# A retention layer's values and gates as one Strassen product whose weight sums are made by adding loads

## The chip, the cores and the metric

One of the eight cores of a Trainium2 chip runs the whole program. The time is that of the device from the start of an execution to its end, in microseconds (us); each run executes the program once, and the median of three runs is quoted. One further execution was recorded by the hardware profiler, and all rows below are from it. TensorE multiplies, VectorE (DVE) and ScalarE (ACT) do arithmetic on tiles, GpSimd (POOL) does arithmetic more slowly and can issue transfers, SyncE (SP) only issues transfers. On TensorE the profile keeps the loading of the stationary operand (PEld) apart from the matmuls (PE).

## The reference

The model has four layers over 512 tokens of width 1024; each has a token mixer and a feed-forward part. Only the mixer of layer 1, a retention with 4 heads, is touched:

```python
proj = x @ w_in                                   # 1024 -> 6144
q, k = proj[..., :1024], proj[..., 1024:2048]     # 4 heads x 256, both rotated
v = proj[..., 2048:4096]                          # 4 heads x 512
g = proj[..., 4096:]                              # 4 heads x 512
y = (retention_chunked(q, k, v, log_gamma[0], False)
     + flip_seq(retention_chunked(flip_seq(q), flip_seq(k), flip_seq(v), log_gamma[1], True)))
y = (y - mean(y)) * rsqrt(var(y) + eps)           # over the 512 columns of a head
y = y * gn_w + gn_b
return (silu(g) * y) @ w_o                        # 2048 -> 1024
```

All of it is in 32-bit floats.

## The kernel before, in words

Tokens lie in 4 tiles of 128. The layer's input stands transposed in `xh` and `xl`: every 32-bit operand of a product is split into a rounded high part and the rest (`split`, lines 100 to 103: a copy on ScalarE, line 101, and a subtraction on VectorE, line 102), and `mm3` (lines 124 to 128) multiplies two split operands with three matmuls, high by high, and the two mixed ones. A matmul takes 128 rows by 512 columns.

Weights come through `wload` (lines 105 to 113): SP loads 512 KB into one of three `wraw` tiles, and `wsplit` makes `whi` and `wlo`, of which six pairs exist. For 512 columns a tile holds 2 of the 8 blocks of the inner dimension.

Per head, `retention` does these steps, in this order from head 1 on: `queries_keys` (two products of 48 matmuls; the rotation `rope`, lines 778 to 792, is six operations on VectorE and two splits for each), `turn` (line 904: 16 transposes of the gated result of the head before, four splits), `values` (96 matmuls, split as they leave PSUM), `scores` (24 matmuls, the decay on VectorE, splits), `gate` (96 matmuls, Silu on ScalarE), `mix` (line 881: 48 matmuls, then for each token tile the group norm) and `out` (line 915: 96 matmuls with the output weights of the head before, added into the residual `xt`). After head 3, `turn` and `out` are done once more, and the layer norm follows.

The group norm of a tile is statistics on VectorE (lines 893 and 894), a reciprocal root by eight small operations (`rsqrt`, lines 139 to 147), one more small operation (898), the scaling on ScalarE (899), the product with the weights on VectorE (900), and the addition of the bias and the product with the gate on GpSimd (901 and 902).

The order of each engine's instructions is fixed when the program is built. The framework goes by the order of the code, but passes over an instruction whose buffer or operand isn't ready in its own model of the times and takes a later one that is. On the chip every engine runs its instructions in that order, and waits where something is late. Buffers of general use (`b`, 2 KB per partition) are 47 in this layer; PSUM has 6 banks for products and 2 for transposes.

## Time and profile before

| | |
|---|---|
| median of 3 runs | 2554.17 us (2553.12 to 2557.45) |
| the profiled execution, own time | 2556.36 us |
| its span in the profile | 2554.6 us |
| TensorE busy, share of the span | 99% |
| VectorE, ScalarE, GpSimd | 69%, 38%, 8% |
| mean granted clock of TensorE | 0.996 of full |
| retention layer | about 594 to 1028 us of the span |

The own time of the profiled execution counts 1.8 us that lie outside the first and last instruction of the span. Matmuls overlap in the profile, so that the time from the start of one to the start of the next says what each costs, not its duration. An engine's busy share says nothing of when it waits; the timeline does.

### The profile page before, as it was taken

How to read it: one execution, taken by the hardware profiler on the slowest of the kernel's cores; microseconds unless marked ns; L12 is line 12 of the kernel's file. 1: busy time of each engine (PE TensorE's matmuls, PEld its weight loads, DVE VectorE, ACT ScalarE, POOL GpSimd, SP SyncE). 2: the span in 40 equal slices, each digit the busy share in tenths (PEclk: the TensorE clock that was granted, in tenths of full speed). 3: DMA queues.
4: the chain of work that ended last, by engine and by line, in shares of the span. 5: the costliest groups of instructions: out<-in, count | busy, mean ns of one | idle time of the engine just before them, and what ended most of it. 6: DMA issues, size and time to landing. Idle time of an engine off the chain costs nothing.

```text
span 2554.6 us, 32573 instructions
## 1 busy us (share of the span) xinstructions
PE 2528.1 (99%) x12804; PEld 2151.0 (84%) x12804; DVE 1771.5 (69%) x2988; ACT 975.2 (38%) x1405; POOL 200.8 (8%) x247
## 2 busy tenths in 40 slices
PE   8999999999999999999999999999999999999998
PEld 7888888888888888988888899988888888988887
DVE  6887766658655647666657878866657786666656
ACT  4653333323332323333332665233332564233331
POOL 2000111000101101111100000011100100011101
PEclk9999999999999999999999999999999999999999
DMA  4213333323222323333333322333332221333331
GB/s 149 75 42 95 99 105 101 99 83 99 77 89 66 97 94 99 99 99 99 107 99 83 91 73 75 112 99 99 99 91 79 83 67 58 109 99 99 99 91 58
DMA packets 294713, 232.35 MB, mean 91 GB/s; under 512 B 21120, under 2 KB 244480, under 8 KB 294560
## 3 DMA queue, kind: packets, MB, share of 16 engines
q1 hardware_dynamic: 294560, 230.28, 29.9%
q8 instruction: 100, 1.64, 0.3%
q14 instruction: 53, 0.43, 0.1%
HBM read 228.15 MB, written 2.10 MB: 90 GB/s over the span
## 4 chain that ended last, share of the span: by engine, by line
PE 93%; DVE 3%; ACT 2%; DMA 1%; issue 1%; POOL 1%; SPq 0%; DVEq 0%; ACTq 0%
PE ps L126 30%; PE ps L128 30%; PE ps L127 30%; PE tp L658 1%; PE tp L156 1%; DVE wlo L102 1%; PE ps L639 1%; PE ps L638 1%; DMA wraw<-in_mla_w_down 0%; ACT whi L101 0%; DMA wraw<-in_ret_w_in 0%; ACT bh L101 0%; DVE xt L203 0%; DVE lnst L184 0%; DVE xt L180 0%
## 5 line engine op out<-in xcount | busy, mean ns | idle before, releaser
L101 ACT CAST whi<-wraw 128x1024 fp32r<-128x1024 f32 (+3 forms) x398 | 412.0, 1040 | 693.7 <-PE ps L127 228.8
L126 PE MATMUL ps<-xh,whi 128*128 128x512 f32 (+1 forms) x1792 | 656.8, 367 | 0.0
L127 PE MATMUL ps<-xl,whi 128*128 128x512 f32 (+1 forms) x1792 | 656.5, 366 | 0.1
L128 PE MATMUL ps<-xh,wlo 128*128 128x512 f32 (+1 forms) x1792 | 656.4, 366 | 0.0
L102 DVE TENSOR_TENSOR wlo<-wraw,whi 128x1024 fp32r<-128x1024 f32 (+3 forms) x398 | 487.8, 1235 | 211.6 <-ACT whi L101 204.3
L127 PEld LDWEIGHTS ps<-xl,whi 128*128 128x128 f32 x1792 | 337.9, 189 | 55.1 <-DVE lnx L139 0.3
L128 PEld LDWEIGHTS ps<-xh,wlo 128*128 128x128 f32 x1792 | 337.9, 189 | 54.9
L126 PEld LDWEIGHTS ps<-xh,whi 128*128 128x128 f32 x1792 | 337.6, 189 | 55.1 <-issue 0.4
L126 PE MATMUL ps<-whi,xh 128*128 128x512 f32 (+3 forms) x752 | 265.1, 353 | 0.7 <-ACT xh L101 0.7
L128 PE MATMUL ps<-whi,xl 128*128 128x512 f32 (+3 forms) x752 | 263.2, 350 | 1.6 <-DVE xl L102 1.5
L127 PE MATMUL ps<-wlo,xh 128*128 128x512 f32 (+3 forms) x752 | 262.9, 350 | 0.3 <-DVE lnx L139 0.2
L180 DVE TENSOR_TENSOR xt<-ps,xt 128x512 f32<-128x512 f32 x288 | 187.2, 682 | 34.9 <-PE ps L128 34.9
L126 PE MATMUL ps<-whi,fh 128*128 128x512 f32 x448 | 174.3, 389 | 0.0
L127 PE MATMUL ps<-wlo,fh 128*128 128x512 f32 x448 | 174.3, 389 | 0.0
L128 PE MATMUL ps<-whi,fl 128*128 128x512 f32 x448 | 174.3, 389 | 0.0
L128 PEld LDWEIGHTS ps<-whi,xl 128*128 128x128 f32 x752 | 143.2, 190 | 19.9 <-DVE xl L102 2.9
L126 PEld LDWEIGHTS ps<-whi,xh 128*128 128x128 f32 x752 | 143.4, 191 | 18.4 <-ACT xh L101 1.1
L127 PEld LDWEIGHTS ps<-wlo,xh 128*128 128x128 f32 x752 | 143.3, 191 | 17.5 <-DVE wlo L102 0.9
L322 DVE TENSOR_TENSOR ft<-ps,b 128x512 f32<-128x512 f32 x64 | 44.2, 691 | 141.5 <-PE ps L128 77.9
L101 ACT CAST whi<-wt 128x1024 fp32r<-128x1024 f32 x64 | 67.5, 1054 | 191.4 <-PE ps L127 131.3
L325 POOL TENSOR_TENSOR ft<-ft 128x256 f32<-128x256 f32 x32 | 23.6, 736 | 1485.7 <-DVE ft L322 1485.7
L102 DVE TENSOR_TENSOR fl<-ft,fh 128x1792 fp32r<-128x1792 f32 x32 | 64.8, 2026 | 91.4 <-ACT fh L101 91.4
(257 smaller groups left out, 3989.2 us busy)
## 6 DMA issues: line engine op xcount, KB each, us to landing
wraw<-in_ffn_w_in SPq DMA_DIRECT2D x176, 512.0 KB, 3.9
wt<-in_ffn_w_out SPq DMA_DIRECT2D x48, 512.0 KB, 4.7
wraw<-in_ret_w_in SPq DMA_DIRECT2D x48, 512.0 KB, 3.8
wraw<-in_ffn_w_out SPq DMA_DIRECT2D x40, 512.0 KB, 3.3
wraw<-in_gla_w_in SPq DMA_DIRECT2D x22, 512.0 KB, 3.7
wraw<-in_mla_w_o SPq DMA_DIRECT2D x16, 512.0 KB, 3.8
wraw<-in_ret_w_o SPq DMA_DIRECT2D x16, 512.0 KB, 4.9
wraw<-in_mla_w_down SPq DMA_DIRECT2D x8, 512.0 KB, 4.7
```

The lines of the kernel that those rows point to most:

```text
L101: a = self.nc.scalar.copy(hi, src)
L102: b = self.nc.vector.tensor_tensor(lo, src, hi.bitcast(F32), op=ALU.subtract)
L126: mm(out, s[0], m[0], start=start, stop=False)
L127: mm(out, s[0], m[1], start=False, stop=False)
L128: mm(out, s[1], m[0], start=False, stop=stop)
L156: nc.tensor.transpose(ps[:, j, :], self.xt[t][:, (4 * g + j) * P : (4 * g + j + 1) * P], self.ident)
L180: nc.vector.tensor_tensor(x, ps, x, op=ALU.add)
L322: nc.vector.tensor_tensor(ft[:, 2:4, :] if f % 2 else ft[:, 1::-1, :], half(pu), half(s), op=ALU.mult)
L325: tt(ft[:, 4, :], ft[:, 0, :], ft[:, 3, :], op=ALU.add)
L638: nc.tensor.matmul(ps, qr[:, sl], krh, start=False, stop=False)
L639: nc.tensor.matmul(ps, qr[:, sl], krz[e], start=False, stop=True)
L658: nc.tensor.transpose(ps[:, kk, qq, :], pq[qq][:, k * P : (k + 1) * P], self.ident)
```

## The change

In heads 1 to 3, values and gates become one product of a 512 x 1024 by a 1024 x 1024 matrix, cut into 2 x 2 blocks (256 tokens, 512 of the inner dimension, 512 columns; values are the left column of blocks, gates the right one) and done by Strassen's scheme in Winograd's form with seven block products. The sums of blocks of x are made once per layer on VectorE (`factors`). The sums of weight blocks are made by the transfers: SP loads the first block into a scratch tile, and GpSimd issues up to three more transfers that add to it. The output of the head before is given out in eight steps, two after each of the first four products, and the output of head 3 stays last. The group norm is done for two token tiles together, with all of its tile arithmetic on VectorE. The tags of the layer's buffers change to 30 general ones, 8 for the factors and 2 of scratch.

```diff
--- before.py
+++ after.py
@@ -144,6 +144,23 @@
         stt(u, u, -10.0 / 3.0, u, op0=ALU.add, op1=ALU.mult)
         stt(y, u, 5.0, y, op0=ALU.add, op1=ALU.mult)
         stt(u, y, y, m, op0=ALU.mult, op1=ALU.mult)
+        stt(y, u, 0.5625, y, op0=ALU.add, op1=ALU.mult)
+        return y
+
+    def rsqrt_n(self, v, n, eps, tag):
+
+        tt, ts, stt = self.nc.vector.tensor_tensor, self.nc.vector.tensor_scalar, self.nc.vector.scalar_tensor_tensor
+        x, y, u, m = (self.small(n, tag + c) for c in "xyum")
+        c = -27.0 / 1024.0
+        ts(x, v, eps, None, op0=ALU.add)
+        ts(m, x, c, None, op0=ALU.mult)
+        ts(y.bitcast(I32), x.bitcast(I32), -0.5, float(0x5F3759DF), op0=ALU.mult, op1=ALU.add)
+        tt(u, y, y, op=ALU.mult)
+        tt(u, u, x, op=ALU.mult)
+        stt(u, u, -10.0 / 3.0, u, op0=ALU.add, op1=ALU.mult)
+        stt(y, u, 5.0, y, op0=ALU.add, op1=ALU.mult)
+        tt(u, y, y, op=ALU.mult)
+        tt(u, u, m, op=ALU.mult)
         stt(y, u, 0.5625, y, op0=ALU.add, op1=ALU.mult)
         return y
 
@@ -883,23 +900,28 @@
             gb = self.b()
             nc.sync.dma_start(gw, ins["ret_gn_w"][j, h * 512 : (h + 1) * 512].partition_broadcast(P))
             nc.sync.dma_start(gb, ins["ret_gn_b"][j, h * 512 : (h + 1) * 512].partition_broadcast(P))
-            for t in range(NT):
-                ps = self.ps()
-                sl = slice(t * P, (t + 1) * P)
-                for m in range(NT):
-                    self.mm3(ps, (at[m][0][:, sl], at[m][1][:, sl]), v[m], m == 0, m == NT - 1)
-                st = self.small(6, "gnst")
-                mv = self.small(2, "gnmv")
-                nc.vector.bn_stats(st, ps)
-                nc.vector.bn_aggr(mv, st)
-                r = self.rsqrt(mv[:, 1:2], 1.0, LN_EPS, "gn")
-                y = self.b()
-                nb = self.small(1, "gnb")
-                nc.vector.scalar_tensor_tensor(nb, mv[:, 0:1], -1.0, r, op0=ALU.mult, op1=ALU.mult)
-                nc.scalar.activation(y, ps, AF.Identity, bias=nb, scale=r)
-                nc.vector.tensor_tensor(y, y, gw, op=ALU.mult)
-                nc.gpsimd.tensor_tensor(y, y, gb, op=ALU.add)
-                nc.gpsimd.tensor_tensor(gs[t], gs[t], y, op=ALU.mult)
+            for t0 in (0, 2):
+                pss = []
+                mv = self.small(4, "gnmv").rearrange("p (t a) -> p t a", a=2)
+                for t in (t0, t0 + 1):
+                    ps = self.ps()
+                    sl = slice(t * P, (t + 1) * P)
+                    for m in range(NT):
+                        self.mm3(ps, (at[m][0][:, sl], at[m][1][:, sl]), v[m], m == 0, m == NT - 1)
+                    st = self.small(6, "gnst")
+                    nc.vector.bn_stats(st, ps)
+                    nc.vector.bn_aggr(mv[:, t - t0, :], st)
+                    pss.append(ps)
+                r = self.rsqrt_n(mv[:, :, 1], 2, LN_EPS, "gn")
+                nb = self.small(2, "gnb")
+                nc.vector.scalar_tensor_tensor(nb, mv[:, :, 0], -1.0, r, op0=ALU.mult, op1=ALU.mult)
+                for t, ps in zip((t0, t0 + 1), pss):
+                    e = t - t0
+                    y = self.b()
+                    nc.scalar.activation(y, ps, AF.Identity, bias=nb[:, e : e + 1], scale=r[:, e : e + 1])
+                    nc.vector.tensor_tensor(y, y, gw, op=ALU.mult)
+                    nc.vector.tensor_tensor(y, y, gb, op=ALU.add)
+                    nc.vector.tensor_tensor(gs[t], gs[t], y, op=ALU.mult)
 
         def turn(gs):
             yT = []
@@ -913,11 +935,143 @@
             return yT
 
         def out(h, yT):
-            last = h == RET_H - 1
-            if last:
-                self.ln_begin(l, 0)
+
+            ch = {}
+
+            def step(t, hf):
+                if t == 0:
+                    rows = wo[h * 512 : (h + 1) * 512]
+                    ch[hf] = [self.wcols(rows, c * 256, 2, hf * 512, 512) for c in range(2)]
+                ps = self.ps()
+                for f in range(4):
+                    w2 = ch[hf][f // 2]
+                    sl = slice(t * P, (t + 1) * P)
+                    self.mm3(
+                        ps, (yT[f][0][:, sl], yT[f][1][:, sl]), (w2[0][:, f % 2, :], w2[1][:, f % 2, :]), f == 0, f == 3
+                    )
+                self.acc(t, hf, ps, ALPHA if h == 0 else None, False)
+
+            return [lambda t=t, hf=hf: step(t, hf) for hf in range(2) for t in range(NT)]
+
+        def out_last(h, yT):
+            self.ln_begin(l, 0)
             st = lambda f, t: (yT[f][0][:, t * P : (t + 1) * P], yT[f][1][:, t * P : (t + 1) * P])
-            self.out_proj(st, wo[h * 512 : (h + 1) * 512], 4, ALPHA if h == 0 else None, last)
+            self.out_proj(st, wo[h * 512 : (h + 1) * 512], 4, None, True)
+
+        def factors():
+
+
+            q = [[[x[:, 4 * c : 4 * c + 4, 256 * a : 256 * a + 256] for x in (self.xh, self.xl)] for c in range(2)] for a in range(2)]
+            (a11, a12), (a21, a22) = q
+            f32 = lambda a: a.bitcast(F32)
+            tt = nc.vector.tensor_tensor
+            scratch = lambda: self.b((P, 4, 256), tag="t", name="xs")
+
+            def both(x, y):
+                d, e = scratch(), scratch()
+                tt(d, f32(x[0]), f32(y[0]), op=ALU.subtract)
+                tt(e, f32(x[1]), f32(y[1]), op=ALU.subtract)
+                tt(d, d, e, op=ALU.add)
+                return d
+
+            def keep(d):
+                pr = self.bpair((P, 4, 256), tag="s")
+                self.split(*pr, d)
+                return pr
+
+            d = both(a21, a22)
+            s1 = keep(d)
+            for x in a11:
+                tt(d, d, f32(x), op=ALU.subtract)
+            s2 = keep(d)
+            for x in a12:
+                tt(d, d, f32(x), op=ALU.add)
+            s4 = keep(d)
+            return s1, s2, keep(both(a11, a21)), s4, a11, a12, a22
+
+        def values_gate(h, fac):
+
+
+
+            rows = w.rearrange("(g a p) c -> g p a c", g=4, p=P)
+            s1, s2, s3, s4, a11, a12, a22 = fac
+            v, gs = [None] * NT, [None] * NT
+            tmp = {}
+
+            def load(blocks, c):
+
+                src = [rows[2 * (ac // 2) + c, :, :, 2048 + ac % 2 * 2048 + h * 512 :][:, :, :512] for ac in blocks]
+                if len(blocks) == 1:
+                    t = self.wp.tile([P, 2, 512], F32, tag="wraw", name="wraw", bufs=self.nraw)
+                else:
+                    t = self.b((P, 2, 512), name="wt", tag="t")
+                nc.sync.dma_start(t, src[0])
+                for x in src[1:]:
+                    nc.gpsimd.dma_start(t, x, accum_op=ALU.add)
+                return self.wsplit(t, 2, 512)
+
+            def product(blocks, s, put):
+                ws = [load(blocks, c) for c in range(2)]
+                for tt in range(2):
+                    ps = self.ps()
+                    for k in range(4):
+                        hi, lo = ws[k // 2]
+                        s2_ = tuple(x[:, k, tt * P : (tt + 1) * P] for x in s)
+                        self.mm3(ps, s2_, (hi[:, k % 2, :], lo[:, k % 2, :]), k == 0, k == 3)
+                    put(tt, ps)
+
+            tt_ = nc.vector.tensor_tensor
+
+            def keep(name):
+                def put(tt, ps):
+                    tmp[name, tt] = self.b()
+                    nc.scalar.copy(tmp[name, tt], ps)
+
+                return put
+
+            def put_v(t, x):
+                v[t] = self.bpair()
+                self.split(*v[t], x)
+
+            def put6(tt, ps):
+                u = tmp["u", tt] = self.b()
+                tt_(u, ps, tmp["c11", tt], op=ALU.add)
+                x = tmp["c21", tt]
+                tt_(x, x, u, op=ALU.add)
+
+            def put2(tt, ps):
+                x = tmp["c11", tt]
+                tt_(x, ps, x, op=ALU.add)
+                put_v(tt, x)
+
+            def put5(tt, ps):
+                u = tmp["u", tt]
+                tt_(u, ps, u, op=ALU.subtract)
+
+            def put3(tt, ps):
+                g = gs[tt] = self.b()
+                tt_(g, ps, tmp["u", tt], op=ALU.add)
+                nc.scalar.activation(g, g, AF.Silu)
+
+            def put7(tt, ps):
+                x = tmp["c21", tt]
+                tt_(x, ps, x, op=ALU.add)
+                put_v(2 + tt, x)
+                g = gs[2 + tt] = tmp["u", tt]
+                tt_(g, g, ps, op=ALU.subtract)
+                nc.scalar.activation(g, g, AF.Silu)
+
+            b11, b12, b21, b22 = range(4)
+            steps = [
+                ([b21, b22, b12, b11], a22, keep("c21")),
+                ([b11], a11, keep("c11")),
+                ([b22, b12, b11], s2, put6),
+                ([b21], a12, put2),
+                ([b12, b11], s1, put5),
+                ([b22], s4, put3),
+                ([b12, b22], s3, put7),
+            ]
+            return v, gs, [lambda a=a: product(*a) for a in steps]
 
         for h in range(RET_H):
             if h == 0:
@@ -928,19 +1082,22 @@
                 q, k = queries_keys(h)
                 gs = gate(h)
                 at = scores(h, q, k, gam)
+                gam = decay(1)
+                fac = factors()
             else:
                 q, k = queries_keys(h)
                 yT = turn(gs)
-                v = values(h)
                 at = scores(h, q, k, gam)
                 gam = decay(h + 1) if h + 1 < RET_H else None
-                gs = gate(h)
-            if h == 0:
-                gam = decay(1)
+                v, gs, todo = values_gate(h, fac)
+                outs = out(h - 1, yT)
+                for step in todo:
+                    step()
+                    for _ in range(2):
+                        if outs:
+                            outs.pop(0)()
             mix(h, at, v, gs)
-            if h:
-                out(h - 1, yT)
-        out(RET_H - 1, turn(gs))
+        out_last(RET_H - 1, turn(gs))
 
 
     def gla(self, l, j):
@@ -1245,7 +1402,7 @@
         return yT
 
     def mixer(self, i):
-        with self.phase(**({}, {}, {"v": 8, "r": 4})[i % 3]):
+        with self.phase(**({}, {"s": 8, "t": 2, "b": 30}, {"v": 8, "r": 4})[i % 3]):
             (self.mla, self.retention, self.gla)[i % 3](i, i // 3)
 
     def before(self, i, eng):
```

## Rows read from the trace of the kernel before

**Rows 1.** The page: span, then busy time, share and instructions.

```profile
span 2554.6 us, 32573 instructions
PE 2528.1 (99%) x12804; PEld 2151.0 (84%) x12804; DVE 1771.5 (69%) x2988; ACT 975.2 (38%) x1405; POOL 200.8 (8%) x247
```

**Rows 2.** Busy time by stretch: one head, and part of head 0.

```profile
core 0: us, PE busy (x) PEld busy (x) DVE busy (x) ACT busy (x) POOL busy (x), PEclk, DMA share, GB/s
805.00:910.00 105.00, 105.00 (x472) 87.04 (x471) 61.79 (x111) 34.98 (x43) 10.30 (x8) 1.00 0.30 91
600.00:668.00 68.00, 67.28 (x305) 55.51 (x304) 43.50 (x87) 26.86 (x34) 2.60 (x2) 1.00 0.37 109
```

**Rows 3.** Timeline of TensorE at the end of head 3: start, length, line, tile.

```profile
973.80 0.39 PE L128 MATMUL ps<-bh,bl 128*128 128x512 f32 x1
974.03 0.39 PE L126 MATMUL ps<-whi,bh 128*128 128x512 f32 x1
...
995.56 0.39 PE L128 MATMUL ps<-whi,bl 128*128 128x512 f32 x1
995.79 1.03 PE L909 MATMUL tp<-ident,b 128*128 128x128 f32 x8
997.07 0.50 PE L126 MATMUL ps<-whi,bh 128*128 128x512 f32 x1 [0.24 <-ACT bh L101]
...
1001.56 0.48 PE L128 MATMUL ps<-whi,bl 128*128 128x512 f32 x1
```

**Rows 4.** Timeline of TensorE in head 3 from the keys to the values.

```profile
912.07 0.39 PE L128 MATMUL ps<-xh,wlo 128*128 128x512 f32 x1
912.30 1.03 PE L909 MATMUL tp<-ident,b 128*128 128x128 f32 x8
913.09 0.48 PE L126 MATMUL ps<-whi,xh 128*128 128x512 f32 x1
```

**Rows 5.** Timeline of VectorE in head 3: rotation of the keys, first and last.

```profile
912.50 0.69 DVE L787 TENSOR_TENSOR b<-ps,tab 128x512 f32<-128x512 f32 x1 [2.11 <-PE ps L128]
...
918.27 0.69 DVE L102 TENSOR_TENSOR bl<-b,bh 128x512 fp32r<-128x512 f32 x1 [0.69 <-ACT bh L101]
```

**Rows 6.** Timelines of VectorE and GpSimd: group norm of head 3.

```profile
967.80 0.69 DVE L893 BATCH_NORM_STATS2 gnst<-ps 128x6 f32<-128x512 f32 x1
...
971.75 0.68 DVE L900 TENSOR_TENSOR b<-b 128x512 f32<-128x512 f32 x1
...
986.21 1.29 POOL L902 TENSOR_TENSOR b<-b 128x512 f32<-128x512 f32 x1
```

**Rows 7.** Groups by line in two heads (700 to 910 us): busy, mean ns.

```profile
L102 DVE TENSOR_TENSOR wlo<-wraw,whi 128x1024 fp32r<-128x1024 f32 x33 | 40.2, 1223 | 41.5 <-ACT whi L101 40.8
L146 DVE SCALAR_TENSOR_TENSOR gnu<-gny,gnm 128x1 f32<-128x1 f32 x8 | 6.2, 777 | 0.2
L900 DVE TENSOR_TENSOR b<-b 128x512 f32<-128x512 f32 x8 | 5.5, 688 | 1.8 <-ACT b L899 1.8
L101 ACT CAST whi<-wraw 128x1024 fp32r<-128x1024 f32 x32 | 33.7, 1054 | 58.5 <-PE ps L128 22.9 <-PE ps L127 21.3 <-DMA wraw<-in_ret_w_in 7.3
```

**Rows 8.** Transfers: queue 1; two loads, us to landing; SP's waits.

```profile
q1 hardware_dynamic: 294560, 230.28, 29.9%
...
wraw<-in_ret_w_o SPq DMA_DIRECT2D x16, 512.0 KB, 4.9
...
DMA to landing us min/median/max: 3.5/3.8/8.4
...
SPq L110 <- DVE wlo L102: 184.5, 31, 26.1
```

**Rows 9.** A gap on TensorE; then stretches, columns as in rows 2.

```profile
72.92 0.39 PE L128 MATMUL ps<-bh,wlo 128*128 128x512 f32 x1
76.38 0.79 PE L126 MATMUL ps<-bh,whi 128*128 128x512 f32 x1 [3.06 <-ACT whi L101]
...
75.00:80.00 5.00, 3.62 (x9) 2.85 (x10) 3.95 (x6) 2.27 (x3) 0.00 (x0) 0.53 0.43 107
80.00:85.00 5.00, 5.00 (x19) 4.01 (x18) 3.17 (x8) 3.44 (x6) 0.00 (x0) 0.79 0.50 158
```

## The prediction

> **What bounds the kernel now.** I read the shares of the engines first [rows 1]: TensorE is busy for 2528.1 of 2554.6 us, so a change counts only by the matmul time that it removes and by the idle time that it opens on TensorE. GpSimd, at 8%, has room. Then I read one head of the retention layer by itself [rows 2]: in 105 us TensorE runs 472 instructions without a gap, which are the 456 matmuls (96 for queries and keys, 96 values, 96 gates, 24 scores, 48 for mixing, 96 for the output) and 16 transposes of a head. VectorE is busy for 61.8 us of it, ScalarE for 35.0, the 16 DMA engines for 30%. Last I read the order on TensorE at the two places where the change takes a neighbour away: the end of the last head [rows 3] and the step from keys to scores [rows 4]. Matmuls there start 0.227 us apart (973.80 to 974.03), and this spacing, not the 0.39 us of one, is the price of a matmul.
>
> **The change, part by part.**
>
> Matmuls removed. Values and gates of a head take 8 block products of 24 matmuls; Strassen's scheme takes 7. That is 24 fewer per head, 72 in heads 1 to 3: 72 x 0.227 = **16.3 us** saved, all on the engine that sets the end.
>
> VectorE and ScalarE. Per head there are 14 weight tiles to split in place of 8: 6 x 1.223 = 7.3 us more on VectorE and 6 x 1.054 = 6.3 on ScalarE [rows 7]. The combinations are 14 operations of 512 columns, at the 0.688 us of line 900 [rows 7] 9.6 us. Eight additions and products come over from GpSimd, 8 x 0.688 = 5.5. The paired square root issues some 22 small operations in place of 36; the costliest of them averages 0.777 us now because some of its runs stand beside GpSimd's arithmetic [rows 6, 7], so I take 7 us back. VectorE goes from 62 to about 77 us in a head of 99.6 us (105 less 5.4), ScalarE from 35 to 44. Both stay below TensorE, so I cost this at nothing. If that cover were gone, each microsecond of VectorE over the head would count. The factors of x, made once during head 0, are 14 operations of 1.22 us, 17 us, in a stretch where VectorE is busy for 43.5 of 68 us [rows 2]; nothing too. They hold the two scratch tiles that the first summed weights need, so head 1's first product can't begin to load before they are done.
>
> SP's queue. 14 plain loads per head in place of 8, at 0.4 us to issue. SP waited 184.5 us of 210 for free tiles [rows 8]: nothing. The buffers of general use fall from 47 to 30; I count at most 28 alive (8 each for queries with keys, scores and turned outputs, and 4 in passing), so nothing, but the loads of the group norm's weights can no longer run far ahead.
>
> GpSimd's queue. 14 adding transfers of 512 KB per head, which the trace of before doesn't have: its queue is all SP's [rows 8]. Each waits for the transfer before it into the same tile, and behind it wait all later additions on GpSimd, then the split on ScalarE and VectorE. The plain load of this size lands after 3.5 us at best and 8.4 at worst, median 3.8 or 4.9 [rows 8]. These are my two ends; an addition also reads what it adds to, so a gain is excluded, and I take 4.9, the slower of the medians. In a head the chain of tiles is four sums deep (3, 2, 1, 1 additions, two tiles each): strictly one after another 14 x 4.9 = 69 us, and four times a first load and a split, 4 x (3.8 + 2.3) = 24, together 93 us in a head of 99.6. With the two tiles of a product in flight together it is some 60 us. It fits both ways, so I cost it at nothing; one after another it stops fitting from (99.6 - 24) / 14 = 5.4 us per addition, in pairs from 10.8.
> The Trainium skill (Collectives: The Full Stack, section on why ReduceScatter is half of AllGather) says that a reducing transfer reads two sources and so moves at half the rate. At the 301 GB/s of queue 1 (230.28 MB in 29.9% of the span) that adds 1.7 us to 3.8, an estimate of 5.5 us, by which the strict order would just not fit: 101 us. No run here shows an adding transfer.
>
> Output of the head before. Its 96 matmuls move from behind the mixing to between the products. For heads 1 and 2 the queries and keys of the next head (96 matmuls, 21.8 us) then follow the mixing, which covers the group norm as before. **For head 3 nothing follows.** Now [rows 3], the last mixing matmul starts at 973.80, the output of head 2 runs to 995.56, and only then come the transposes of head 3. After the change TensorE must wait for the whole group norm of the last pair of tiles. From the statistics to the first product with the weights now takes 971.75 - 967.80 = 3.95 us [rows 6], in which 0.6 us is another tile's statistics and to which two operations (0.4) come: 3.8. Then six operations of about 0.62 (two tiles, three each), 3.7; a transpose, 0.3; the copy of its result, 0.7; and 0.5 from the last matmul to the statistics: 9.0 us. If the statistics of the last tile queue behind the first pair's six operations, 1.9 more. TensorE is idle 9 to 11 us. Part of this was paid before: from 995.79 to 1001.56 it ran 13 matmuls (2.9 us) and lost 2.8 on transposes and waits, of which about 1 stays. So the end of the layer costs 7.2 to 9.1 us; I take **8.2**.
>
> The clock behind that idle time. After the 3.45 us between the starts at 72.92 and 76.38 us the granted clock is 0.53 of full in that stretch of 5 us and 0.79 in the next [rows 9]: matmuls ran at the lower level, 1.2 GHz, at first and lost 0.47 x 3.6 (to 80 us) + 0.21 x 5 = **2.7 us**. The cost can't be below 0, and no row stands behind a longer gap in mid-kernel; I take 2.7 as measured, with 0 as the lower end and twice that as the upper one.
>
> Small waits. The values' second half comes out of the last product just before the mixing reads it, and head 1's first sums start late. Bounds: 0, if ready matmuls of other steps fill them, as the values now fill the wait for a transpose buffer [rows 4]; and 16, if the scores are not filled (below). I take **2**, near the lower end, since rows 4 show the filling.
>
> **Sum:** -16.3 + 8.2 + 2.7 + 2 = -3.4 us. The profiled execution took 2556.4 us for its span of 2554.6, so 2553.0 by its own time; against the median of the runs, 2554.2, from which it lies 2.2 us, that is **2550.8**. A measurement of this kernel can tell about 0.2%, 5.1 us, from no change.
>
> **Rivals.**
> A. *The last wait is short.* If the group norm runs faster without GpSimd (its last addition and product end at 987.50, 13.7 us after the mixing [rows 3, 6]) or output work of head 2 is left for the end, the layer's end costs 3 to 5 us with little clock loss: -9, **2545**. For it: each addition on GpSimd took 1.29 us against 0.69. Against: the chain above is counted without GpSimd, and the framework's order takes ready work at once.
> B. *The additions come late* (the other side). One mechanism: the sums queue one after another on GpSimd, at over 5.4 us each. ScalarE and VectorE run in order, so a split that waits holds up the clearing of PSUM too. At 6 us a head's chain is 14 x 6 + 24 = 108, 9 us over the head, 26 in three heads: **2577**. For it: landings up to 8.4 us, and more bytes (18 in place of 8 MB per head). Against: 30% DMA share now, and two tiles that can be summed side by side. The rule of the Trainium skill cited above (Collectives: The Full Stack, same section) leads here: by its estimate the strict order is just over the edge.
> C. *The scores wait.* The values, 96 matmuls, now stand between keys and scores [rows 4]; the rotation of the keys and its split run from 912.50 to 918.96 [rows 5]. The transposes cover 1.6 us; the rest, 5.3 us, three times is 16, **2565**. It comes if the first product's weights are not there to fill. Against: rows 4.
> D. *The matmuls do not get fewer in time*: the products' spacing rises or VectorE becomes the bound locally, and the 16 us are lost: **2563**.
>
> **How the numbers follow.** Forecast 0.46, A 0.22, B 0.18, C 0.09, D 0.05. The forecast's own range is -8 to +1 us, 2546 to 2555; some 0.28 of it is past -5.1. Faster: 0.13 of the forecast and 0.20 of A, **0.33**. Same: the forecast's other 0.33, 0.02 of A, and 0.02 of mild forms of B and C, **0.37**. Slower: what is left of B, C and D, **0.30**. The range reaches from A's better end, 2543, to B's 2577; beyond lie about 0.08 below and 0.10 above.
>
> **What would show it.** In the profile after: 72 fewer matmuls; head to head about 99.8 us in place of 105.2; GpSimd with no arithmetic in the layer, and 42 adding transfers whose landing I put at 4.9 us; VectorE at some 77 us per head; one idle stretch of 9 to 11 us on TensorE behind the last mixing, ended by VectorE through the transposes, with the granted clock near 0.5 behind it. Wrong would be: idle TensorE inside the heads that a weight split or a GpSimd transfer ends (B), waits at the scores on the keys' copies (C), or no idle stretch at the layer's end (A).

## The result and the profile after

The changed kernel takes 2645.78 us (median of 4 runs, 2643.64 to 2654.1) against 2555.81 for the kernel before in the same series: a ratio of 1.0358, 95% interval 1.0339 to 1.0376. It is slower by 90 us, where I forecast 3 us less. In the runs below the kernel before has medians of 2553.65 to 2554.76; ratios are to those.

The page after (span; busy time, share and instructions), which answers to [rows 1]; then the queue of GpSimd and its transfers (queue: packets, MB, share of 16 engines; issue: count, KB, median us to landing), which [rows 8] did not have:

```profile
span 2641.8 us, 32599 instructions
PE 2524.0 (96%) x12732; PEld 2143.8 (81%) x12732; DVE 1827.6 (69%) x3038; ACT 998.7 (38%) x1437; POOL 208.4 (8%) x257
...
q0 software_dynamic: 11424, 22.02, 5.4%
...
wt<-in_ret_w_in POOLq DMA_DIRECT2D x42, 512.0 KB, 6.1
```

The 72 matmuls are gone. TensorE is not busier, but its share has fallen from 99 to 96%. The stretches, with the columns of [rows 2], say where:

```profile
664.00:689.00 25.00, 0.39 (x2) 0.18 (x2) 2.55 (x3) 3.10 (x4) 4.84 (x4) 0.56 0.59 103
689.00:795.00 106.00, 104.14 (x453) 84.96 (x454) 76.76 (x130) 41.13 (x51) 11.22 (x9) 0.97 0.61 148
795.00:820.00 25.00, 1.09 (x4) 0.50 (x2) 3.24 (x5) 2.10 (x3) 4.87 (x4) 0.61 0.61 108
820.00:928.00 108.00, 104.14 (x447) 84.75 (x446) 72.79 (x121) 39.84 (x50) 12.21 (x10) 0.95 0.66 159
928.00:953.00 25.00, 0.45 (x2) 0.03 (x1) 2.83 (x4) 1.91 (x4) 4.84 (x4) 0.61 0.62 113
```

Three stretches of 25 us, one at the mixing of each of heads 0, 1 and 2 (in heads 1 and 2 six of its matmuls have run), have almost no TensorE. In them no engine works much: VectorE and ScalarE some 3 us each, GpSimd four instructions. The second one on TensorE:

```profile
795.03 0.39 PE L128 MATMUL ps<-bh,bl 128*128 128x512 f32 x1
819.33 1.22 PE L126 MATMUL ps<-bh 128*128 128x512 f32 x2 [23.91 <-ACT bh L101]
...
822.55 0.63 PE L126 MATMUL ps<-bh 128*128 128x512 f32 x1
825.64 0.80 PE L126 MATMUL ps<-bh 128*128 128x512 f32 x1 [2.46 <-ACT bh L101]
```

TensorE waits for `bh`, a copy on ScalarE of head 1's values. ScalarE in the same time, and the operation on VectorE that makes the copy's operand:

```profile
793.52 1.06 ACT L101 CAST whi<-wraw 128x1024 fp32r<-128x1024 f32 x1 [3.53 <-DMA wraw<-in_ret_w_in]
817.72 1.04 ACT L101 CAST whi<-wt 128x1024 fp32r<-128x1024 f32 x1 [23.14 <-DMA wt<-in_ret_w_in]
818.67 0.61 ACT L101 CAST bh<-b 128x512 fp32r<-128x512 f32 x1
819.19 0.62 ACT L1062 ACTIVATE b<-b 128x512 f32<-128x512 f32 x1
824.02 1.04 ACT L101 CAST whi<-wt 128x1024 fp32r<-128x1024 f32 x1 [4.21 <-DMA wt<-in_ret_w_in]
...
795.75 0.68 DVE L1058 TENSOR_TENSOR b<-ps,b 128x512 f32<-128x512 f32 x1
```

The copy takes 0.61 us and its operand was made at 795.75. It stands in ScalarE's order behind the split of `wt`, the **next** head's four-block sum, which head 1 doesn't need at all. And GpSimd, where that sum is made (three additions for each of two tiles):

```profile
708.06 1.22 POOL L1010 DMA_DIRECT2D wt<-in_ret_w_in  x1 [5.06 <-issue]
745.22 1.40 POOL L1010 DMA_DIRECT2D wt<-in_ret_w_in  x1 [35.94 <-DMA wt<-in_ret_w_in]
...
784.62 1.21 POOL L1010 DMA_DIRECT2D wt<-in_ret_w_in  x1 [10.51 <-DVE b L1049]
792.62 1.22 POOL L1010 DMA_DIRECT2D wt<-in_ret_w_in  x1 [6.79 <-issue]
798.94 1.21 POOL L1010 DMA_DIRECT2D wt<-in_ret_w_in  x1 [5.10 <-issue]
805.29 1.22 POOL L1010 DMA_DIRECT2D wt<-in_ret_w_in  x1 [5.14 <-issue]
811.63 1.21 POOL L1010 DMA_DIRECT2D wt<-in_ret_w_in  x1 [5.12 <-issue]
817.93 1.22 POOL L1010 DMA_DIRECT2D wt<-in_ret_w_in  x1 [5.09 <-issue]
```

Six additions, from the second on 6.3 us apart, each issued only when the one before has landed, though two tiles take turns. The gap of 35.94 us ahead of them is as telling: GpSimd has nothing to add to, because SP's first load waits for a scratch tile.

The three stalls are 25.0, 24.3 and 25.1 us from start to start, with 3.1 and 3.0 behind the latter two: some 79 us of idle time after taking off five normal spacings of 0.227. The remainder is the clock that they leave behind, 0.97 and 0.95 of full over the heads that follow.

The end of the layer answers to [rows 3, 6, 9]: TensorE, then the last operation of the group norm on VectorE, then the stretch behind the wait.

```profile
1072.32 0.39 PE L128 MATMUL ps<-bh,bl 128*128 128x512 f32 x1
1074.43 0.95 PE L931 MATMUL tp<-ident,b 128*128 128x128 f32 x4 [1.72 <-DVE b L924]
1081.82 1.29 PE L931 MATMUL tp<-ident,b 128*128 128x128 f32 x4 [6.44 <-DVE b L924]
...
1081.08 1.29 DVE L924 TENSOR_TENSOR b<-b 128x512 f32<-128x512 f32 x2
...
1074.00:1084.00 10.00, 2.57 (x9) 1.42 (x10) 7.59 (x22) 2.52 (x4) 0.00 (x0) 0.64 0.04 13
1084.00:1094.00 10.00, 10.00 (x43) 8.30 (x43) 5.63 (x12) 1.18 (x3) 0.00 (x0) 0.85 0.00 0
```

That is the idle stretch of the forecast, in its place and a little shorter: 1.72 + 6.44 = 8.2 us of waits, where I had 9 to 11. The step to the scores [rows 4] has 1.28 us of wait, which I had taken as filled:

```profile
724.96 1.04 PE L931 MATMUL tp<-ident,b 128*128 128x128 f32 x8
727.28 0.50 PE L126 MATMUL ps<-bh 128*128 128x512 f32 x1 [1.28 <-ACT bh L101]
```

### The profile page after: what moved, and what is told of

It is laid out like the page before. It is cut to its first block, busy times and chain, and to the rows that moved or that the text cites. A ratio compares the mean times of both kernels' runs of the same rounds, so it can differ in the third digit from the quotient of the medians.

```text
span 2641.8 us, 32599 instructions
## 1 busy us (share of the span) xinstructions
PE 2524.0 (96%) x12732; PEld 2143.8 (81%) x12732; DVE 1827.6 (69%) x3038; ACT 998.7 (38%) x1437; POOL 208.4 (8%) x257
## 4 chain that ended last, share of the span: by engine, by line
PE 87%; DVE 4%; issue 3%; DMA 2%; ACT 2%; POOL 1%; DVEq 0%; SPq 0%; ACTq 0%
PE ps L126 28%; PE ps L127 28%; PE ps L128 28%; DMA wt<-in_ret_w_in 2%; PE tp L675 1%; DVE wlo L102 1%; DMA wraw<-in_mla_w_down 1%; PE tp L173 1%; ACT whi L101 1%; PE ps L656 1%; PE ps L655 1%; POOL wt L1010 0%; ACT bh L101 0%; DVE xt L220 0%; ACT b L565 0%
## 5 line engine op out<-in xcount | busy, mean ns | idle before, releaser
L126 PE MATMUL ps<-whi,xh 128*128 128x512 f32 (+3 forms) x632 | 218.2, 346 | 0.7 <-ACT xh L101 0.7
L128 PE MATMUL ps<-whi,xl 128*128 128x512 f32 (+3 forms) x632 | 216.1, 342 | 2.6 <-DVE xl L102 2.6
L127 PE MATMUL ps<-wlo,xh 128*128 128x512 f32 (+3 forms) x632 | 215.8, 341 | 0.1
L126 PE MATMUL ps<-bh 128*128 128x256 f32 (+1 forms) x376 | 127.8, 348 | 83.6 <-ACT bh L101 83.3
L101 ACT CAST whi<-wt 128x1024 fp32r<-128x1024 f32 x88 | 92.6, 1052 | 303.3 <-PE ps L127 134.1
L102 DVE TENSOR_TENSOR wlo<-wt,whi 128x1024 fp32r<-128x1024 f32 x88 | 114.1, 1300 | 121.0 <-ACT whi L101 120.2
L126 PE MATMUL ps<-whi,bh 128*128 128x512 f32 (+1 forms) x416 | 157.1, 378 | 0.5 <-ACT bh L101 0.5
L127 PE MATMUL ps<-wlo,bh 128*128 128x512 f32 (+1 forms) x416 | 156.5, 376 | 0.0
L128 PE MATMUL ps<-whi,bl 128*128 128x512 f32 (+1 forms) x416 | 155.9, 375 | 0.0
L126 PEld LDWEIGHTS ps<-bh 128*128 128x128 f32 x376 | 72.9, 196 | 97.8 <-ACT bh L101 89.6
```

The costliest lines, as they stand in the source:

```text
L101: a = self.nc.scalar.copy(hi, src)
L102: b = self.nc.vector.tensor_tensor(lo, src, hi.bitcast(F32), op=ALU.subtract)
L126: mm(out, s[0], m[0], start=start, stop=False)
L127: mm(out, s[0], m[1], start=False, stop=False)
L128: mm(out, s[1], m[0], start=False, stop=stop)
```

## The experiments

Theory: the additions are late and hold up, through in-order queues, work that has nothing to do with them. Rivals: Strassen's own vector work, the DMA engines that the additions take, and VectorE. All runs change the kernel after, unless another is named.

**Without additions, and with additions that nobody waits for.** For `no_adds` the two lines that add are deleted; for `junk` they add into a tile of their own:

```diff
                 for x in src[1:]:
-                    nc.gpsimd.dma_start(t, x, accum_op=ALU.add)
+                    nc.gpsimd.dma_start(junk, x, accum_op=ALU.add)
```

> Left out: the 42 adding loads; every product is given only the first of its blocks, so the sums are not made. Theory (a sum that is late holds ScalarE's queue, and behind it the copies that the mixing waits for): the three stalls of 24 to 25 us ahead of the mixings of heads 0, 1 and 2 go, with the low clock behind them, and what stays is the 72 matmuls less (-16) and the idle time at the end of the layer (+9 to +12): 2548 to 2558. Rival (the vector work and the order of Strassen's scheme cost the time, not the additions): at least half of the 90 us stays, 2600 or more.

> The 42 adding loads run, but into a tile that nothing reads (4 KB, taken from the pool of 2-KB tiles); every product is given only the first of its blocks. They follow each other without a pause, some 265 us in heads 0 to 3. Theory (what the additions cost is the wait for their sums): nobody waits for them, so within 6 us of the kernel without additions, 2550 to 2560. Rival (they cost by the DMA engines that they take: 3.4 us of each engine for one addition against 1.7 for a plain load of the same size, so that all loads land later): 2575 or more.

`no_adds` takes 2553.59 us, a ratio of 1.0001 (0.9992 to 1.0011). Everything that the change costs is in the additions, 92.2 us, and everything else in it nets to nothing. Span by span the account closes: 2641.8 - 2550.4 = 91.4 us, of which 11.9 are the longer time of TensorE for the same matmuls (2524.0 against 2512.1), at the lower clock, and 79.5 more idle time, the size of the three stalls. Strassen's vector work is all still there (VectorE 1827.2 us, against 1827.6), so that rival falls, and that of VectorE with it:

```profile
span 2550.4 us, 32529 instructions
PE 2512.1 (98%) x12732; PEld 2136.8 (84%) x12732; DVE 1827.2 (72%) x3038; ACT 1000.1 (39%) x1437; POOL 158.0 (6%) x215
...
698.00:800.00 102.00, 100.71 (x451) 82.79 (x450) 76.06 (x124) 41.67 (x53) 0.00 (x0) 1.00 0.39 119
...
765.76 1.05 ACT L101 CAST whi<-wt 128x1024 fp32r<-128x1024 f32 x1 [1.86 <-issue]
766.72 0.62 ACT L101 CAST bh<-b 128x512 fp32r<-128x512 f32 x1
```

Without the additions the framework builds an order that differs in some places from that of the changed kernel, but not in this one: the last two rows are the same split, still ahead of the same copy, and now it holds the copy for at most 1 us. The place alone does no harm; a late sum in that place does.

`junk` takes 2554.56 us, ratio 1.0001 (0.9992 to 1.0010).

```profile
junk<-in_ret_w_in POOLq DMA_DIRECT2D x42, 512.0 KB, 6.2
```

The same 42 transfers, 6.2 us to landing (median), cost nothing when nobody waits for them. The rival of the DMA engines falls.

**One addition at a time: room or the chip?** `ring2048` gives GpSimd's queue 2048 bytes of scratch in place of 1024 (and one 2-KB tile less in two pools); every engine's order is the same. `plain` keeps the 42 transfers, and every engine's order, but lets them overwrite. The line of `ring2048`:

```diff
-    nc = bacc.Bacc("TRN2", target_bir_lowering=False, num_devices=1, dynamic_dma_scratch_size=1024)
+    nc = bacc.Bacc("TRN2", target_bir_lowering=False, num_devices=1, dynamic_dma_scratch_size=2048)
```

> Nothing left out; the scratch of GpSimd's queue is 2048 instead of 1024 bytes (and one 2-KB tile less in two pools), the order of every engine is the same. If additions to the two tiles of one sum are held apart by room in the queue's ring: they go in pairs, six take about 20 us instead of 38, each of the three stalls shrinks by 12 to 18 us, 2590 to 2610. If each addition takes GpSimd or the memory 6.3 us whatever the room: no change, 2643 to 2649.

> The 42 loads on GpSimd's queue stay where they are, but overwrite the tile in place of adding to it, so each product is given only its last block. If the adding makes the load last 6.1 us (the tile read as well as the block): landing near the 4.4 us of SyncE's loads of the same size, issues under 5 us apart, six in 28 us instead of 38, 2600 to 2620. If GpSimd's queue makes it (descriptors, room in the ring), adding or not: 6.0 us or more to landing, issues 6.3 us apart, 2640 to 2650.

`ring2048`: 2610.25 us, 35.5 less. The stalls are 17.5, 13.5 and 13.2 us. GpSimd ahead of the first of them, two additions at a time:

```profile
656.82 2.43 POOL L1010 DMA_DIRECT2D wt<-in_ret_w_in  x2 [7.48 <-DMA wt<-in_ret_w_in]
663.21 1.22 POOL L1010 DMA_DIRECT2D wt<-in_ret_w_in  x1 [3.96 <-DMA wt<-in_ret_w_in]
667.37 1.20 POOL L1010 DMA_DIRECT2D wt<-in_ret_w_in  x1 [2.94 <-DMA wt<-in_ret_w_in]
```

The release is now the landing of an earlier addition to the same tile, not "issue". So the queue's room had kept the two tiles apart. `plain`: 2586.06 us, less than I expected from either side, with stalls of 11.2, 6.8 and 7.3 us. Its queue and transfers:

```profile
q0 software_dynamic: 6048, 22.02, 2.7%
...
wt<-in_ret_w_in POOLq DMA_DIRECT2D x42, 512.0 KB, 4.7
...
656.64 1.49 POOL L1010 DMA_DIRECT2D wt<-in_ret_w_in  x2 [5.98 <-DMA wt<-in_ret_w_in]
```

The same bytes take 144 packets each in place of 272, land in 4.7 us in place of 6.1, and occupy a DMA engine for 0.027 x 2585.6 / 42 = 1.7 us in place of 0.054 x 2641.8 / 42 = 3.4. And two are in flight at once, as the last row shows, for 64 us in all, though the scratch is 1024 bytes; in the changed kernel the trace never has two. That it is the smaller number of packets that leaves room for the second is likely, but I did not test it alone.

**Who stands behind the sum.** `order1` exchanges the first two products, so that the next head's first split needs a plain block; `late` ties the splits of each four-block sum behind the group norm of the mixing before; `order1_ring` is `order1` with the larger scratch. The lines of `order1` and of `late`, where `self.mixed` holds the last two instructions of that group norm:

```diff
             steps = [
-                ([b21, b22, b12, b11], a22, keep("c21")),
                 ([b11], a11, keep("c11")),
+                ([b21, b22, b12, b11], a22, keep("c21")),
```
```diff
-                return self.wsplit(t, 2, 512)
+                if len(blocks) < 4:
+                    return self.wsplit(t, 2, 512)
+                with self.tc.issue_after(self.mixed[0]), self.tc.issue_after(self.mixed[1]):
+                    return self.wsplit(t, 2, 512)
```

> Nothing left out; the first two products of a head change places, so that the next head's first split needs a block that SyncE loads plainly, and the sum of four blocks is split only after the mixing. Theory (head-of-line wait on ScalarE): the additions last as long as before, 6.3 us apart, but nothing that the mixing needs stands behind them: the three stalls go, 2550 to 2565. Rival (six additions one after another, 38 us, are late wherever they stand, and some product waits for them): 2600 or more, with the stall moved to the product of the four-block sum.

> Nothing left out; ScalarE's and VectorE's splits of each four-block sum are tied behind the group norm of the mixing before. Theory (head-of-line wait on ScalarE): as with the products exchanged, the stalls ahead of the three mixings go; the product of the sum may wait a little in their place: 2550 to 2575. Rival (the late sum itself is what TensorE lacks): the stall moves to that product at full size, 2630 or more.

> Nothing left out; the first two products change places and the scratch is 2048 bytes, both edits at once. Theory (two causes in a row: additions one at a time, and a late sum at the head of ScalarE's queue): with nothing of the mixing behind a sum, and additions in pairs, the stalls of 8 to 9.5 us at the four-block and three-block sums go too, 2556 to 2572. Rival (the additions take bandwidth from all loads of a head, whatever their order): as much as with one edit alone, 2595 or more.

`late` 2587.29, `order1` 2605.23, `order1_ring` 2596.60 us: 58, 41 and 49 us less, and all three short of what I expected: `late` lies between its two ranges, the others in those of their rivals. The stalls of 25 us are gone in each. At the mixings of heads 1 and 2 in `late` 3.2 and 4.2 us are left; the second row is the copy that waited behind the split before, and now waits only for its operand:

```profile
781.46 0.50 PE L126 MATMUL ps<-bh 128*128 128x512 f32 x1 [2.85 <-ACT bh L101]
...
780.79 0.62 ACT L101 CAST bh<-b 128x512 fp32r<-128x512 f32 x1 [1.89 <-DVE b L1062]
```

So the place in ScalarE's queue, with a late sum in it, was what made them. But other stalls appear, of 5.2 to 5.5 us in `late` and 5.5 to 9.5 us in the other two. In `order1_ring`, SP, ScalarE, VectorE and TensorE in head 1:

```profile
703.33 29.84 SPq L1008 DMA_DIRECT2D wt<-in_ret_w_in  x4
...
730.47 1.04 ACT L101 CAST whi<-wt 128x1024 fp32r<-128x1024 f32 x1 [8.86 <-DMA wt<-in_ret_w_in]
...
731.54 1.23 DVE L102 TENSOR_TENSOR wlo<-wt,whi 128x1024 fp32r<-128x1024 f32 x1 [8.67 <-ACT whi L101]
...
733.29 0.68 DVE L879 SCALAR_TENSOR_TENSOR b<-ps,ret_g 128x512 f32<-128x512 f32 x1
...
734.03 0.80 PE L126 MATMUL ps<-whi,xh 128*128 128x512 f32 x1 [5.44 <-DVE b L879]
```

Another split of a sum has come to the head of ScalarE's queue. VectorE's part of it is late with it, behind it stands the operation that clears a bank of PSUM, and TensorE waits for that bank. SP's four issues span 29.84 us, with later weights behind them in its queue. Is it the order, then, or the number of additions? `plain_first_ring` puts two plain products ahead of the first sum:

```diff
                 ([b11], a11, keep("c11")),
+                ([b21], a12, put2),
                 ([b21, b22, b12, b11], a22, keep("c21")),
                 ([b22, b12, b11], s2, put6),
-                ([b21], a12, put2),
```

> Nothing left out; scratch of 2048 bytes, all fourteen additions, but the two products of one plain block that can go early stand first, so the four-block sum has 22 us more before its product. Theory (order: a late sum holds what is queued behind it on ScalarE and SyncE): no stall over 3 us, 2556 to 2575. Rival (fourteen additions of 6 us and two scratch tiles are too many for a head in any order): the stall goes on to the three-block sum behind it, 2588 or more.

2610.33 us: in the rival's range. With fourteen additions, two scratch tiles and the larger scratch, none of three orders of the products comes within 40 us of the kernel before; the stall only changes place (here 9.2 and 8.4 us at two mixings, and 1 to 3 us at several products). No run has a third scratch tile, or `late` with the larger scratch, so it is not shown that fourteen additions can't be had cheaper.

**Fewer additions.** The sums are nested: b12+b11, then b22 more, then b21 more. `nested` orders the products so that one tile is added to step by step, 8 additions a head in place of 14, with a plain product first. `nested_dve` loads each further block plainly and adds on VectorE. In the list, a block without brackets is added to the tile that stands there:

```diff
             steps = [
                 ([b11], a11, keep("c11")),
                 ([b12, b11], s1, keep("u")),
                 (b22, s2, put6),
                 ([b21], a12, put2),
                 (b21, a22, put4),
                 ([b22], s4, put3),
                 ([b12, b22], s3, put7),
             ]
```

> Nothing left out; scratch of 1024 bytes as in the changed kernel. The products are put in an order in which each sum is the one before with one block more, in the same tile: 8 additions a head instead of 14, and the first product needs a block alone. Theory: additions last 8 x 6.3 = 50 us of a head instead of 88, none stands ahead of the mixing's copies, no stall over 5 us: 2552 to 2566. Rival (each further block has to wait until the split before has read the tile, so the sums are late one by one): stalls of 6 us or more at three products of each head, 2600 or more.

> Nothing left out; nested sums as before, but each further block is loaded plainly by SyncE into a raw tile and added by VectorE. Per sum tile 1.2 us of VectorE in place of an adding load of 6.1 us; 24 additions are 29 us of VectorE over three heads. Theory (the adding load's length is what is left of the loss of the nested kernel): 2550 to 2562. Rival (VectorE, or the raw tiles that SyncE waits for, become what the heads wait for): 2568 or more, like the nested kernel or worse.

`nested` takes 2568.80 us, just above the expected range, with no stall over 3.1 us inside the heads: 77 of the 92 us are recovered. A plain product first, by itself, had left 2605.23 (`order1`), so 36 of them came with the nested sums. `nested_dve` takes 2560.41 (ratio 1.0026, 1.0016 to 1.0035), in its range.

**The end of the layer.** In the next runs output tiles of head 2 are kept back: four behind head 3's mixing in `nested_ring_cover`; in the runs named "spread", heads 1 and 2 give out two tiles after each of the first two and of the last two products, and head 3 two after each of the first two, one after the last, and three behind its mixing. `no_adds_spread` does it without the additions.

```diff
-                for step in todo:
+                for step, n in zip(todo, (2, 2, 0, 0, 0, 0, 1) if h == RET_H - 1 else (2, 2, 0, 0, 0, 2, 2)):
                     step()
-                    for _ in range(2):
-                        if outs:
-                            outs.pop(0)()
+                    for _ in range(n):
+                        outs.pop(0)()
             mix(h, at, v, gs)
+            if h == RET_H - 1:
+                for o in outs:
+                    o()
```

> Nothing left out; nested sums, scratch of 2048 bytes, and four of the eight output tiles of head 2 kept back until after head 3's mixing. Theory: besides the stalls, the 9 us of idle TensorE and the 3 us of low clock at the end of the layer go, so that the 72 matmuls less are left as a gain: 2540 to 2552, under the kernel before. Rival (the end of the layer waits for the group norm whatever stands before it): within 3 us of the nested kernel.

> Left out: the 42 adding loads; every product is given only the first of its blocks. The output tiles stand as in the run beside it. It bounds what Strassen's scheme can give here with sums for nothing: 16 us of matmuls less and the end of the layer covered, 2537 to 2546. If the idle time at the end of the layer is the group norm's and not to be covered by output tiles: 2550 to 2556, as without additions.

> Nothing left out; the sums on VectorE, and the output tiles of the head before moved among the products: two after each of the first two products and of the last two, so that two stand ahead of the mixing, and for head 3 three stand behind its mixing. Theory: they cover the 2 to 3 us in front of each mixing and the 9 us of idle TensorE with 3 us of low clock at the end of the layer, so the 72 matmuls less show: 2538 to 2550. Rival (weights of the output tiles held longer keep the products' weights out of the six tiles for splits): no faster than with the output tiles where they were, 2552 or more.

`nested_ring_cover` 2559.12 us (1.0017, 1.0007 to 1.0026), 9.7 less than `nested` for two edits at once but above the expected range; `no_adds_spread` 2543.83 (0.9959, 0.9946 to 0.9973); `nested_dve_spread` 2554.23 (0.9999, 0.9990 to 1.0008), a miss by 4 and in its rival's range. Without additions the end of the layer is worth 2553.59 - 2543.83 = 9.8 us: in the traces its waits of 1.72 and 6.44 us become one of 1.2, the other waits of TensorE in the layer stay as they were, and TensorE is busy for 2.3 us less (2512.1 against 2509.8), which is the clock. With sums for nothing, 2544 is the best of these runs. In `nested_dve_spread` 4.0 and 3.6 us lie ahead of the scores of two heads, where the nested kernels with adding loads have 1.6. Two more runs, `nested_pool_spread` with the sums on GpSimd's arithmetic and `nested_ring_spread` with sums by adding loads and the larger scratch:

> Nothing left out; like nested_dve_spread, but the 24 sums are made by GpSimd's arithmetic (a 128x512 addition of it took 1.33 us in the kernel before, so some 2.7 us each here) in place of VectorE's. Theory (what is left of the loss is VectorE's queue ahead of the scores): those 2 to 2.4 us at two heads go, 2545 to 2552. Rival (GpSimd's sums come later than VectorE's or hold VectorE up): 2554 or more.

> Nothing left out; nested sums by adding loads with a scratch of 2048 bytes and the output tiles spread as in nested_dve_spread. Theory: with 8 additions a head in pairs, and two output tiles ahead of each mixing to cover a late split, what is left is small: 2546 to 2555. Rival (a tile of the sum can only be added to once its split has read it, so 6 us a step still show): 2557 or more.

2553.74 (0.9997, 0.9988 to 1.0006) and 2552.05 us (0.9994, 0.9985 to 1.0003). GpSimd's additions took 2.4 to 3.3 us each. The first misses its range by 1.7 us: the gaps ahead of the scores are still 3.6 and 2.4 us. Its trace says why. Although 24 additions of 1.2 us had left VectorE, it is busy for 1857.6 us, more than in `nested_dve_spread` (1850.7). In the layer every elementwise operation of VectorE from SBUF to SBUF that starts while GpSimd adds ends only after that addition. So does the last operation of a rotation, ahead of the scores, while GpSimd adds from 802.04 to 804.76:

```profile
803.79 1.52 DVE L805 TENSOR_TENSOR b<-b 128x512 f32<-128x512 f32 x1
```

It takes 0.69 us where GpSimd is idle; a subtraction of the splits goes up to 2.9, also from 0.69. The rotation's operations that read PSUM keep their 0.68. So the sums left VectorE, and VectorE waits for them instead. The second run lies in its range. The last two put two (`nrs2`) and three (`nrs3`) output tiles between head 3's last product and its mixing, by (2, 1, 0, 0, 0, 0, 2) and (2, 0, 0, 0, 0, 0, 3) in the line above.

> Nothing left out; nested_ring_spread with two output tiles in place of one between head 3's last product and its mixing (one fewer earlier on). Theory: the waits of 2.4 and 1.6 us in front of that mixing go and the clock behind them stays: 4 to 6 us under nested_ring_spread, 2545 to 2549. Rival (the mixing waits for a split that is late for another reason, such as weights held longer): within 2 us of nested_ring_spread, 2550 to 2555.

> Nothing left out; three output tiles there. Theory: as with two, no more is to be had, 2545 to 2549; if the wait was not covered with two, it is with three. Rival: the four tiles' weights are held over five products and the products' own weights come late: 2551 or more.

2550.78 (0.9990, 0.9982 to 0.9999) and 2550.27 us (0.9980, 0.9971 to 0.9989). The waits of 2.4 and 1.6 us at that mixing are gone in both traces, but the gain of 4 to 6 us is not there: they take 1.3 and 1.8 us less than `nested_ring_spread`, so by size the rivals were nearer. In their place TensorE now waits earlier, at head 3's last product: from start to start 1.3 us in `nrs2`, 1.4 and 1.3 us in `nrs3`, for the split of a sum that waits for an addition to land. In `nrs3`:

```profile
954.01 0.50 PE L126 MATMUL ps<-whi,bh 128*128 128x512 f32 x1 [1.00 <-ACT whi L101]
...
952.91 1.04 ACT L101 CAST whi<-wt 128x1024 fp32r<-128x1024 f32 x1 [4.98 <-DMA wt<-in_ret_w_in]
```

So the additions still show a little. `nrs3` is the fastest version that leaves nothing out, 0.2% under the kernel before.

## Why the prediction was wrong

**The step that failed** is the pricing of GpSimd's queue: "It fits both ways, so I cost it at nothing." The additions cost 92.2 us. Three things in it were off.
- *The size.* I took 4.9 us per addition; the median is 6.1, and 6.3 from issue to issue. I had written that the strict order stops fitting at 5.4. The Trainium skill (Collectives: The Full Stack, section on why ReduceScatter is half of AllGather), from which I had the estimate of 5.5 us, was the nearer guide. Its rule, two reads for each byte written, stated there for the reduce step of a collective, agrees with the runs here: twice the time of each DMA engine, 3.4 us against the 1.7 of `plain`. The rule says nothing of the wait for the queue.
- *The order in flight.* I left open whether two tiles are summed side by side. With 1024 bytes of scratch they are not: the trace never has two additions in flight.
- *The comparison.* I set a head's whole chain, 93 us, against a head's whole time, 99.6. With the measured 6.3 us it gives 14 x 6.3 + 24 = 112, 13 us over, 38 in three heads: less than half of the loss. What counts is the time from when a scratch tile comes free to when the first instruction **behind** the split is wanted. For the four-block sum SP could load the first tile at 778.59, and the copy behind its split was wanted at 796, with TensorE ready at 795: some 17 us. The sum took 39, to 817.72, and the other tile's until 824.02. The two chains also take turns: the sum waits for a tile that the previous split must have read, the splits wait for the sum. GpSimd stood idle for 35.94 us before, and SP waited in the layer for tiles to be split and for additions to land, as its issue of the two loads and its waits say:

```profile
778.59 5.58 SPq L1008 DMA_DIRECT2D wt<-in_ret_w_in  x2
...
SPq L1008 <- DVE wlo L102: 189.6, 40, 20.4
SPq L1008 <- DMA wt<-in_ret_w_in: 77.7, 8, 21.4
```

An average that fits says nothing about a deadline.

**Rival B had the mechanism**, in-order queues and a split that waits on ScalarE, with 0.18 and a price of 26 us. The price was too small by a factor of 3.5 for the same reason, and what stood behind the split in the changed kernel was a copy of values, not the clearing of PSUM; that came in `order1_ring`.

**The rest, by `no_adds`.** Matmuls: 72 fewer and 16.0 us of TensorE's busy time (2528.1 - 2512.1), against 16.3. VectorE: 76.1 us in a head, against 77. End of the layer: 8.2 + 2.7 = 10.9 forecast, 9.8 measured by the two runs without additions. The granted clock behind it was 0.64 and 0.85 in two stretches of 10 us. Small waits were too low: heads follow each other in 101.8 us, not 99.8. Of the 2 us, 1.3 are TensorE idle at the scores (100.71 busy in 102), a mild form of rival C; the other 0.7 stays open. Three heads make 6 us, where I had priced 2 for all. So the sum of the other terms came out at 0, interval -2.0 to +2.8 us, in place of -3.4. Rivals A and D did not occur.

## What to carry to other kernels

A prefetch that is late costs more than the thing it feeds: its first consumer blocks everything behind it on an in-order engine, here copies for another head. So price a queue not by its mean load but by each chain's latency against the moment when the instruction behind its consumer is wanted, and let the first step after a busy stretch need only a plain load. Where partial sums are wanted, nest them, so that each costs one addition; and keep some independent TensorE work for behind a long vector chain.

## What the runs showed of the hardware that I had not expected

An adding transfer of 512 KB is 272 packets and 6.1 us, a plain one from the same queue 144 packets and 4.7 us, one from SP 4.2. It takes twice the DMA engines' time (3.4 us of each, against 1.7), and yet 42 of them, one after another, left the time of the kernel as it was (`junk`).

The scratch of GpSimd's queue bounds how many such transfers are in flight: one with 1024 bytes, with issues 6.3 us apart; two with 2048, worth 35.5 us here for the price of a 2-KB tile. Whether 2048 would hold more is not shown, as there are two tiles to add to. The Trainium skill (DMA: Bandwidth & Descriptors, section SWDGE vs HWDGE vs iDMA) says that these descriptors are written by GpSimd into rings that live in a part of SBUF set aside; the two runs agree, in that with more scratch more are in flight; where the descriptors lie, no run here shows.

GpSimd's additions hold up VectorE's elementwise operations from SBUF to SBUF (0.69 us became 1.52 in the row of `nested_pool_spread`, and up to 2.9), but not those that read PSUM (0.68).
